# Hybrid decoder layer on one core: the gate and branch products turned round to 512 columns, with a clamp moved to ScalarE and a tile moved in SBUF

## The chip, the core and the metric

The kernel runs on one core of a Trainium2 chip. The metric is the device time of one execution in microseconds (us), the median of several runs. The profile names the engines as follows: PE is TensorE (matrix products) and PEld its weight loads, DVE is VectorE, ACT is ScalarE, POOL is GpSimd, and SP is SyncE, which here only issues DMAs. "L198" is line 198 of the kernel before.

## What is computed

The input is `x` with 256 tokens of 1024 channels. The layer is a SwiGLU feed-forward block, a mixer, and a second SwiGLU block, each with an RMSNorm in front and behind. The change lies in the mixer:

```python
u = rmsnorm(h, mix_pre_g)
z, xbc, dt_raw, q, k, v, gate_logits = jnp.split(u @ w_in, IN_SPLITS, axis=-1)
y_ssd = ssd_branch(z, xbc, dt_raw, ...)      # Mamba-2, ends in y @ ssd_w_branch  (2048 -> 1024)
y_att = diff_attn_branch(q, k, v, ...)       # ends in out @ da_w_branch          (1024 -> 1024)
gates = jax.nn.sigmoid(gate_logits + gate_b).reshape(b, L, 2, D_MODEL)
merged = gates[:, :, 0] * y_ssd + gates[:, :, 1] * y_att
h = h + rmsnorm(merged @ w_out, mix_post_g)
```

Inside `ssd_branch` the decay between two tokens of a chunk is `exp(a_cum[l] - a_cum[s])` for `s <= l` and zero otherwise. The kernel clamps the exponent at zero, so that the masked half can't overflow, and masks by a multiplication afterwards.

## The kernel before

**Precision and products.** Every large product is done in three: both operands are split into a rounded high part and the remainder (`hi`, `lo`, type fp32r), and hi·hi, hi·lo and lo·hi are summed in PSUM. Weights come in as chunks of 1 MB, listed at the top in the order of use (L86 to L132). `load_to` issues the loads on SP into three buffers `raw`. `split_steps` (L147) splits a chunk: ScalarE writes `whi` (L164) and VectorE `wlo` (L165), in four tiles. `take` (L177) hands out the next chunk and traces the splits of the chunks up to two ahead.

**Memory.** Most tiles of 4 KB a partition share one pool, `k4`, with 29 buffers. The normed input `u` has its own two buffers (tag `u8`). PSUM has eight banks: three for `pj`, the accumulators of products, and five for `bg`, used by everything smaller and by the four accumulators of a down projection (`acc_mx`, `acc_f`).

**Two forms of product.** `mm_t` (L191) keeps a 128x128 piece of the weights in the array and streams the 256 tokens, so the result has channels on partitions: 48 matmuls of 256 columns a chunk of 1024x256. `mm_nat` (L221) keeps 128 tokens of the activation in the array and streams 512 weight columns, so the result has tokens on partitions: 12 matmuls of 512 columns for a block of 128 tokens and a chunk of 512x512. Before the change the gates, both branches, and the projections to x, z, q and k use `mm_t`; V and the first columns of each feed-forward block use `mm_nat`. `mm_n` (L418) is the down projection: weights of 256 rows and 1024 columns, streamed 512 columns at a time, with the merged activations as stationary operand. Its first chunk is used at once for both token blocks, its last three are held and used block by block.

**Order.** From L1042 on PE runs in the order in which the program is written (`own_order(PE)`); the other engines are ordered by the framework's scheduler, in program order as far as operands are ready by its own model of time. `Background` (L976) feeds the smaller work between the large products: each generator yields what a step is priced at, `run(us)` adds to an account and issues steps until it is spent, and a `BREAK` ends a run. The steps are those of `ssd_work` (L769, the decays E and the products py), `ssd_norm` (L809) and `att_work` (L951, eight heads in four pairs; `Pair.turn`, L934, transposes a pair's output and splits it to `oh` and `ol`). Runs are placed after each product of z, q and k (`BG_US`, 2.8) and at each half chunk of the gates and of the SSD branch (`SLOT_US`, 1.55).

**The tail of the mixer.** Gates (L1047 to L1065): product, bias and eviction on ScalarE (L1056), then one switch of the activation table to the sigmoid and back. SSD branch (L1069 to L1077): product, VectorE multiplies by the gate (L1076). Attention branch (L1084 to L1105): the first chunk's product waits for three of four pairs, runs six of its eight K tiles, drains the background (with the last pair's transposes), and then goes on; VectorE multiplies by the gate and adds (L1096 to L1100); `split` writes `mh` and `ml`, which are already in the form in which `mm_n` wants them (channels on partitions). Then come `acc_mx` (L1107), `mm_n` (L1115) and the second feed-forward block.

Of the kernel before, what the change touches and what calls it, by code (L numbers as in the profile page):

```python
# [15 lines left out]
F32R = mybir.dt.float32r  # L16
# [22 lines left out]
WARM = 6  # L39
FILL = 8  # L40
TAIL = 3
BG_US = 2.8
SLOT_US = 1.55
BREAK, STOP = object(), object()


# [1 line left out]
def tile_hybrid_layer(ctx: ExitStack, tc: tile.TileContext, x, ffn1_pre_g, ffn1_w_gate, ffn1_w_up,  # L48
# [10 lines left out]
    def k4(shape, name, dt=F32):  # L59
        return sb.tile(shape, dt, tag="k4", name=name, bufs=K4_BUFS)  # L60
# [17 lines left out]
    def pjt(name):  # L78

        return pj(name).rearrange("p (m t) -> p m t", m=2)  # L80
# [7 lines left out]
    def t_chunk(w, k0, c0):  # L88
        chunks.append((w[k0:k0 + D, c0:c0 + T].rearrange("(j p) c -> p j c", p=P), [P, KD, T]))
# [30 lines left out]
    for c in range(4):  # L120
        t_chunk(w_in2, 0, Q0 + c * T)
        t_chunk(w_in2, 0, KK0 + c * T)
    for c in range(8):
        t_chunk(w_in2, 0, G0 + c * T)
    for c in range(4):
        t_chunk(ssd_w_branch[0], 0, c * T)
        t_chunk(ssd_w_branch[0], D, c * T)
    for c in range(4):
        t_chunk(da_w_branch[0], 0, c * T)
    for c in range(4):  # L130
        n_chunk(w_out[0], c * 2 * P)
    ffn_chunks(ffn2_w_gate, ffn2_w_up, ffn2_w_down)  # L132
# [55 lines left out]
        nc.scalar.copy(hi, src)  # L188
        nc.vector.tensor_sub(lo, src, hi.bitcast(F32))

    def mm_t(acc, w, act, k0=0, first=True, last=True, slot=None, ks=range(KD)):  # L191

        (wh, wl), (ah, al, _) = w, act
        acc = acc if isinstance(acc, list) else [acc[:, m, :] for m in range(2)]
        for m in range(2):
            cs = slice(m * P, (m + 1) * P)
            for j in ks:
                nc.tensor.matmul(acc[m], wh(j)[:, cs], ah(k0 + j), start=first and j == ks[0], stop=False)  # L198
                nc.tensor.matmul(acc[m], wh(j)[:, cs], al(k0 + j), start=False, stop=False)  # L199
            for j in ks:  # L200
                nc.tensor.matmul(acc[m], wl(j)[:, cs], ah(k0 + j), start=False, stop=last and j == ks[-1])  # L201
            if slot and m == 0:
                slot()

    def mm_w(dst, name, w, act):

# [45 lines left out]
    def own_order(*engines):  # L252

        if not ordered[0]:
            order_of[0].enter_context(tc.manual_schedule(engines=set(engines)))
            ordered[0] = True
# [43 lines left out]
    cols_a = const.tile([P, P], F32, name="cols_a")  # L300
    col, gain_rows = {}, []
    row = 0
    for name, v in (("mx", mix_pre_g), ("f2", ffn2_pre_g), ("gb", gate_b),
                    ("ng", ssd_norm_g), ("cb", ssd_conv_b), ("sg", da_subln_g)):
        n = v.shape[1] // P
        gain_rows.append((row, n, v))
        col[name] = row
        row += n
# [106 lines left out]
        nc.gpsimd.dma_start(pg, v[0].partition_broadcast(P))  # L415
        return pg

    def mm_n(acc, acts, ready, turned):  # L418


        n = len(acts) // 2
        held = []

        def one(i, w, parts):
            wh, wl = w
            for kt in range(2):
                ah, al = acts[2 * i + kt]
                for b, qs in parts:
                    ts = slice(b * P, (b + 1) * P)
                    for x_, w_ in ((ah, wh), (al, wh), (ah, wl)):  # L430
                        for q in qs:
                            nc.tensor.matmul(acc[b][q], x_[:, ts], w_(kt)[:, halves[q]],  # L432
                                             start=i == 0 and kt == 0 and x_ is ah and w_ is wh,
                                             stop=i == n - 1 and kt == 1 and w_ is wl)

        for i in range(n):
            w = take()
            if i < n - TAIL:
                one(i, w, ((0, (0, 1)), (1, (0, 1))))
            else:  # L440
                held.append((i, w))
        own_order(PE)
        for q in range(2):
            for i, w in held:
                one(i, w, ((0, (q,)),))
        ready(0)
        for q in range(2):
            for i, w in held:
                if q == 1 and i == n - TAIL:
                    turned()  # L450
                one(i, w, ((1, (q,)),))
        split_to(taken[0] + AHEAD)
        ready(1)
# [268 lines left out]
    nc.tensor.matmul(pac[:, 288:320], tri, av[:, 1, :], start=True, stop=True)  # L722
    nc.tensor.matmul(pac[:, 320:352], after_m, av[:, 0, :], start=True, stop=True)
    acT = k2([H_SSD, T], "acT")
    nc.scalar.copy(acT, pac[:H_SSD, :T])
    acs = const.tile([P, 3, H_SSD], F32, name="acs")
    nc.scalar.copy(acs, pac[:, 256:352].rearrange("p (a h) -> p a h", a=3))
    acd = dram.tile([H_SSD, T], F32, name="acd")
# [40 lines left out]
    def ssd_work(groups):  # L769
        for g in groups:  # L770
# [10 lines left out]
            for hf in range(2):  # L781
# [4 lines left out]
                for pr in range(2):  # L786
                    E = k3([P, 2, 3 * P], f"E{g}{hf}{pr}")
                    for i in range(2):
                        hd = r0 + pr * 2 + i
                        lh = pr * 2 + i  # L790
                        nc.vector.tensor_scalar(E[:, i, :P], acb[:, lh, P:], acs[:, 1, hd:hd + 1], 0.0,
                                                ALU.subtract, ALU.min)
                        nc.vector.tensor_scalar(E[:, i, P:T], acb[:, lh, :P], acs[:, 0, hd:hd + 1], 0.0,
                                                ALU.subtract, ALU.min)
                        act(E[:, i, T:], acb[:, lh, P:], AF.Exp, bias=acs[:, 2, hd:hd + 1])
                    act(E[:, :, :T], E[:, :, :T], AF.Exp)
                    nc.vector.tensor_tensor(E, E, cbm[g].unsqueeze(1).to_broadcast([P, 2, 3 * P]), ALU.mult)
                    c = hf * 2 + pr
                    for i in range(2):
# [115 lines left out]
    class Pair:  # L915
# [18 lines left out]
        def turn(self):  # L934
            hp = self.hp
            pt = bg([P, 4, P], f"pto{hp}")
            for i in range(4):
                nc.tensor.transpose(pt[:, i, :], self.o[:, i, :], ident)
            if hp % 2 == 0:
                oh[hp // 2] = k4([P, 4, T], f"oh{hp}", F32R)  # L940
                ol[hp // 2] = k4([P, 4, T], f"ol{hp}", F32R)
            o = (hp % 2) * 2
            turned_pairs[0] += 1
            hi, lo = (w[hp // 2][:, o:o + 2, :].rearrange("p i t -> p (i t)") for w in (oh, ol))
            pt = pt.rearrange("p i t -> p (i t)")
            nc.scalar.activation(hi, pt, AF.Identity, scale=g8)
            nc.vector.scalar_tensor_tensor(lo, pt, g8, hi.bitcast(F32), ALU.mult, ALU.subtract)

# [92 lines left out]

    own_order(PE)  # L1042

    def slot():
        back.run(SLOT_US)

    def gates(half):  # L1047
        tiles = []
        for c in range(4):
            if c % 2 == 0:  # L1050
                tiles.append(k4([P, 4, T], f"gt{half}{c}"))
            acc = pjt(f"pgt{half}{c}")
            mm_t(acc, take(), act_u, slot=slot)
            for m in range(2):
                n = col["gb"] + half * 8 + c * 2 + m
                nc.scalar.activation(tiles[-1][:, (c % 2) * 2 + m, :], acc[:, m, :], AF.Identity,  # L1056
                                     bias=cols_a[:, n:n + 1])
            slot()
        return tiles

    gt0, gt1 = gates(0), gates(1)
    act_table(SIGMOID)
    for t in gt0 + gt1:
        act(t, t, AF.Sigmoid)
    act_table(EXP_LN)  # L1065
    while yl[3] is None:
        back.run(0.1)
    act_y = (lambda j: yh[j // 4][:, j % 4, :], lambda j: yl[j // 4][:, j % 4, :], None)
    for c in range(4):  # L1069
        acc = [pj(f"pws{c}{m}")[:, :T] for m in range(2)]  # L1070
        mm_t(acc, take(), act_y, 0, True, False, slot)
        slot()
        mm_t(acc, take(), act_y, KD, False, True, slot)
        for m in range(2):
            t = gt0[c // 2][:, (c % 2) * 2 + m, :]
            nc.vector.tensor_tensor(t, acc[m], t, ALU.mult)  # L1076
        slot()  # L1077
    del act_y
    yh = yl = None
    while turned_pairs[0] < 3:  # L1080
        back.run(0.1)
    act_o = (lambda j: oh[j // 4][:, j % 4, :], lambda j: ol[j // 4][:, j % 4, :], None)

    w0, acc0 = take(), [pj(f"pwd0{m}")[:, :T] for m in range(2)]  # L1084
    mm_t(acc0, w0, act_o, 0, True, False, slot, range(6))
    slot()
    back.drain()
    act_table(SILU)
    mg = []
    for c in range(4):  # L1090
        acc = pjt(f"pwd{c}") if c else acc0
        mm_t(acc, w0 if c == 0 else take(), act_o, 0, c > 0, True, None, range(KD) if c else range(6, KD))
        cs = slice((c % 2) * 2, (c % 2) * 2 + 2)
        t0, t1 = gt0[c // 2][:, cs, :], gt1[c // 2][:, cs, :]
        if c:
            nc.vector.tensor_tensor(t1, acc, t1, ALU.mult)  # L1096
        else:
            for m in range(2):
                nc.vector.tensor_tensor(t1[:, m, :], acc[m], t1[:, m, :], ALU.mult)
        nc.vector.tensor_tensor(t1, t1, t0, ALU.add)  # L1100
        if c % 2 == 0:
            mh = k4([P, 4, T], f"mh{c}", F32R)
            ml = k4([P, 4, T], f"ml{c}", F32R)
        split(mh[:, cs, :], ml[:, cs, :], t1)
        mg += [(mh[:, cs.start + m, :], ml[:, cs.start + m, :]) for m in range(2)]  # L1105
    pg = load_gain(mix_post_g, "pg_mx")
    acc = [[bg([P, 512], f"acc_mx{b}{q}") for q in range(2)] for b in range(2)]  # L1107

# [3 lines left out]
        post_norm(b, acc[b], pg, 1.0, "mxp")  # L1112
        ready(b)

    mm_n(acc, mg, mixed, turned)  # L1115


    ov = out[0].rearrange("(b p) d -> p b d", p=P)
# [42 lines left out]
```

## Time and profile before

| | us |
|---|---|
| median of 3 runs (759.28 to 759.61) | 759.56 |
| the profiled execution, its time | 759.13 |
| the profiled execution, its span from the first to the last instruction | 757.4 |

| stretch of the span (us) | what runs in it on PE |
|---|---|
| 246 to 295 | x projection, with the convolution |
| 295 to 407 | z, q and k projections, with the decays, py and the SSD norm between |
| 407 to 461 | gates, with SSD norm and heads 0 to 3 between |
| 461 to 518 | SSD branch, with heads 4 to 7 between |
| 518 to 543.5 | attention branch |
| 543.5 to 566 | down projection `acc_mx` and the norm before the second feed-forward block |

Durations are those of one profiled execution. Consecutive matmuls overlap (their starts lie closer together than their listed durations), so their pace is read from the chain of work, where each piece is charged only with what it adds. A busy share of an engine is a sum of listed durations.

### The profile page before, as it was taken

Reading aid. Unit: us, or ns where it says so; the run is one execution under the profiler, and the core shown is the slowest. Engines: PE = TensorE matmul, PEld = TensorE weight load, DVE = VectorE, ACT = ScalarE, POOL = GpSimd, SP = SyncE. Lnnn points to the kernel's source line nnn. Section 1 sums busy time; section 2 is a strip of 40 time slices with the busy share of each in tenths; the row PEclk is TensorE's granted clock in tenths of the full one; section 3 lists DMA queues with packets and bytes.
Section 4 is the critical chain, followed back from the end, with each engine's and each line's share of the span. In section 5 each row is a group of like instructions: output and inputs, shape, how many; then the busy total and the mean of one; then the engine's idle time right before and its main releaser. Section 6 shows DMA issues by size and latency. Waiting matters only on the chain.

```text
span 757.4 us, 11973 instructions
## 1 busy us (share of the span) xinstructions
PE 746.9 (99%) x4841; PEld 670.7 (89%) x4841; DVE 524.0 (69%) x819; ACT 436.0 (58%) x716; POOL 39.0 (5%) x75
## 2 busy tenths in 40 slices
PE   8999999999999999999999999999999999999996
PEld 7888888888889999899999999999988888888885
DVE  6686567664577888887877866975884867766612
ACT  7465557553656565666846768654573756664511
POOL 6400000000200000000000000000010000000000
PEclk9999999999999999999999999999999999999999
DMA  9685666576253738465645663543671667544701
GB/s 319 156 280 158 212 222 245 188 263 221 63 167 114 223 117 269 146 221 173 189 117 163 189 201 112 177 156 114 222 250 56 222 223 221 169 172 184 283 0 56
DMA packets 104200, 136.99 MB, mean 181 GB/s; under 512 B 2668, under 2 KB 88784, under 8 KB 104144
## 3 DMA queue, kind: packets, MB, share of 16 engines
q1 hardware_dynamic: 101728, 129.51, 52.0%
q0 software_dynamic: 2112, 6.18, 2.7%
q8 instruction: 38, 0.62, 0.3%
q10 hardware_dynamic: 304, 0.53, 0.2%
q14 instruction: 18, 0.15, 0.1%
HBM read 135.13 MB, written 1.08 MB: 180 GB/s over the span
## 4 chain that ended last, share of the span: by engine, by line
PE 96%; DVE 1%; POOL 1%; ACT 1%; DMA 1%; issue 0%; SPq 0%; DVEq 0%; POOLq 0%; ACTq 0%
PE acc_f L432 16%; PE pup_f L215 9%; PE pg_f L215 9%; PE pn_f L230 5%; PE pg_f L214 4%; PE pup_f L214 4%; PE pn_mx L230 3%; PE acc_mx L432 3%; PE pws L198 2%; PE pgt L198 2%; PE pxs L201 2%; PE pws L201 2%; PE pxs L199 2%; PE pgt L201 2%; PE pxs L198 2%; PE pgt L199 2%
## 5 line engine op out<-in xcount | busy, mean ns | idle before, releaser
L165 DVE TENSOR_TENSOR wlo<-raw,whi 128x1024 fp32r<-128x1024 f32 (+1 forms) x246 | 291.9, 1214 | 50.0 <-ACT whi L164 49.1
L164 ACT CAST whi<-raw 128x1024 fp32r<-128x1024 f32 (+1 forms) x246 | 247.1, 1043 | 52.7 <-PE acc_f L432 19.9
L215 PE MATMUL pg_f<-u_f,whi 128*128 128x512 f32 x288 | 101.2, 396 | 0.0
L215 PE MATMUL pup_f<-u_f,whi 128*128 128x512 f32 x288 | 101.1, 396 | 0.0
L214 PE MATMUL pg_f<-u_f,wlo 128*128 128x256 f32 x252 | 70.5, 280 | 0.0
L214 PE MATMUL pup_f<-u_f,wlo 128*128 128x256 f32 x252 | 70.3, 279 | 0.0
L215 PEld LDWEIGHTS pg_f<-u_f,whi 128*128 128x128 f32 x288 | 52.9, 188 | 9.7
L215 PEld LDWEIGHTS pup_f<-u_f,whi 128*128 128x128 f32 x288 | 52.7, 188 | 9.8
L432 PE MATMUL acc_f<-whi,gh_f 128*128 128x512 f32 x176 | 58.1, 390 | 0.0
L432 PE MATMUL acc_f<-whi,gl_f 128*128 128x512 f32 x176 | 58.1, 389 | 0.0
L432 PE MATMUL acc_f<-wlo,gh_f 128*128 128x512 f32 x176 | 58.1, 389 | 0.0
L214 PEld LDWEIGHTS pg_f<-u_f,wlo 128*128 128x128 f32 x252 | 47.5, 189 | 1.7
L214 PEld LDWEIGHTS pup_f<-u_f,wlo 128*128 128x128 f32 x252 | 47.5, 189 | 1.6
L219 DVE TENSOR_TENSOR su_f<-pup_f,su_f 128x256 f32<-128x256 f32 x36 | 15.2, 422 | 40.0 <-ACT su_f L218 40.0
L432 PEld LDWEIGHTS acc_f<-wlo,gh_f 128*128 128x128 f32 x176 | 33.0, 188 | 6.9
L432 PEld LDWEIGHTS acc_f<-whi,gl_f 128*128 128x128 f32 x176 | 33.0, 188 | 6.9
L432 PEld LDWEIGHTS acc_f<-whi,gh_f 128*128 128x128 f32 x176 | 33.0, 188 | 6.7
L198 PE MATMUL pgt<-u_mx,whi 128*128 128x256 f32 x128 | 32.5, 291 | 0.0
L198 PE MATMUL pz<-u_mx,whi 128*128 128x256 f32 x128 | 32.3, 288 | 0.0
L198 PE MATMUL pws<-yh,whi 128*128 128x256 f32 x128 | 32.2, 290 | 0.0
L199 PE MATMUL pz<-u_mx,whi 128*128 128x256 f32 x128 | 31.7, 284 | 0.0
L198 PE MATMUL pxs<-u_mx,whi 128*128 128x256 f32 x128 | 31.7, 285 | 0.0
(311 smaller groups left out, 1571.9 us busy)
## 6 DMA issues: line engine op xcount, KB each, us to landing
raw<-in_w_in_dram SPq DMA_DIRECT2D x40, 1024.0 KB, 5.5
raw<-in_ffn_w_down_dram SPq DMA_DIRECT2D x22, 1024.0 KB, 5.4
raw<-in_ffn_w_gate_dram SPq DMA_DIRECT2D x20, 1024.0 KB, 5.9
raw<-in_ffn_w_up_dram SPq DMA_DIRECT2D x20, 1024.0 KB, 5.5
raw<-in_ssd_w_branch_dram SPq DMA_DIRECT2D x8, 1024.0 KB, 5.3
acb<-acd POOLq DMA_DIRECT2D x8, 512.0 KB, 4.3
raw<-in_da_w_branch_dram SPq DMA_DIRECT2D x4, 1024.0 KB, 5.3
raw<-in_w_out_dram SPq DMA_DIRECT2D x4, 1024.0 KB, 5.0
```

The costliest lines, as they stand in the source:

```text
L164: nc.scalar.copy(hi[:, js, :], r[:, q * nj + j:q * nj + j + n, :])
L165: nc.vector.tensor_sub(lo[:, js, :], r[:, q * nj + j:q * nj + j + n, :], hi[:, js, :].bitcast(F32))
L198: nc.tensor.matmul(acc[m], wh(j)[:, cs], ah(k0 + j), start=first and j == ks[0], stop=False)
L199: nc.tensor.matmul(acc[m], wh(j)[:, cs], al(k0 + j), start=False, stop=False)
L201: nc.tensor.matmul(acc[m], wl(j)[:, cs], ah(k0 + j), start=False, stop=last and j == ks[-1])
L214: nc.tensor.matmul(acc[:, :T], wl(j)[:, cs], ah(j), start=False, stop=False)
L215: nc.tensor.matmul(acc, wh(j)[:, cs], ahl(j), start=j == 0, stop=j == KD - 1)
L219: nc.vector.tensor_tensor(dst[:, m, :], acc[:, :T], dst[:, m, :], ALU.add)
L230: nc.tensor.matmul(acc, a(k0 + j), b(j), start=first and i == 0, stop=last and i == 11)
L432: nc.tensor.matmul(acc[b][q], x_[:, ts], w_(kt)[:, halves[q]], start=i == 0 and kt == 0 and x_ is ah and w_ is wh, stop=i == n - 1 and kt ...
```

## The change

Every part is in the mixer.

1. **The products turned round.** Gates, SSD branch and attention branch are computed by `mm_nat` through a new helper `natural`: two accumulators of 128 tokens by 512 channels, a chunk of 512x512 used for block 0 and block 1 in turn, a background run after each. The chunk lists become 512x512 pieces; number and bytes stay as they are.
2. **What follows from it.** The bias of the gates now lies along the free axis, so `gate_b` is broadcast to all partitions by two DMAs on GpSimd's queue (one small load of it at the start goes), and the eviction is an addition on VectorE. The sigmoid stays. Multiplications by the gate have 512 columns. The merged result has tokens on partitions and must be transposed for `mm_n`: `turn_merged` does 4 transposes on PE for each block and half, and splits from PSUM. The first half's are issued after the first chunk of the second half; the second half's inside `mm_n`, through a new argument `begun`, after its first chunk and ahead of the held three.
3. **The clamp.** `acT` is stored negated. For each head one of the two clamps (`tensor_scalar` on VectorE) becomes a `Relu` on ScalarE with the bias operand; the Exp takes scale -1.
4. **Half of `o`.** `oh` and `ol` of pairs 2 and 3 lie in one tile of the `u8` pool, free once the gates are done, in place of two `k4` tiles.
5. **The background's account.** `BG_US` 2.8 becomes 3.15; a run in the gates is worth 1.35; in the SSD branch 1.55 as before. The attention branch waits for two pairs, and drains after its first chunk.

```diff
-BG_US = 2.8
-SLOT_US = 1.55
+BG_US = 3.15
+GATE_US = 1.35
+SSD_US = 1.55
...
-    def mm_n(acc, acts, ready, turned):
+    def mm_n(acc, acts, ready, turned, begun=lambda: None):
...
         own_order(PE)
+        begun()
         for q in range(2):
...
-    nc.scalar.copy(acT, pac[:H_SSD, :T])
+    nc.scalar.activation(acT, pac[:H_SSD, :T], AF.Copy, scale=-1.0)
...
-                        nc.vector.tensor_scalar(E[:, i, :P], acb[:, lh, P:], acs[:, 1, hd:hd + 1], 0.0,
-                                                ALU.subtract, ALU.min)
+                        act(E[:, i, :P], acb[:, lh, P:], AF.Relu, bias=acs[:, 1, hd:hd + 1])
                         nc.vector.tensor_scalar(E[:, i, P:T], acb[:, lh, :P], acs[:, 0, hd:hd + 1], 0.0,
-                                                ALU.subtract, ALU.min)
-                        act(E[:, i, T:], acb[:, lh, P:], AF.Exp, bias=acs[:, 2, hd:hd + 1])
-                    act(E[:, :, :T], E[:, :, :T], AF.Exp)
+                                                ALU.add, ALU.max)
+                        act(E[:, i, T:], acb[:, lh, P:], AF.Exp, bias=acs[:, 2, hd:hd + 1], scale=-1.0)
+                    act(E[:, :, :T], E[:, :, :T], AF.Exp, scale=-1.0)
...
+            elif hp == 2:
+
+                o8 = sb.tile([P, 4, 2, T], F32R, tag="u8", name="o8", bufs=2)
+                oh[1], ol[1] = o8[:, :, 0, :], o8[:, :, 1, :]
...
+    def natural(name, n, hi, lo, evict, us, then=lambda: None):
+
+
+        accs = [pj(f"{name}{b}") for b in range(2)]
+        for i in range(n):
+            w = take()
+            for b in range(2):
+                bs = slice(b * P, (b + 1) * P)
+                mm_nat(accs[b], w, (lambda k: hi(k)[:, bs], lambda k: lo(k)[:, bs]), i * 4, i == 0, i == n - 1, "u")
+                if i == n - 1:
+                    evict(b, accs[b])
+                back.run(us)
+            if i == 0:
+                then()
+
+
+    gt = [[None] * 2 for _ in range(2)]
+    for half in range(2):
+        gb = k4([P, D], f"gb{half}")
+        nc.gpsimd.dma_start(gb, gate_b[0][half * D:(half + 1) * D].partition_broadcast(P))
+        for b in range(2):
+            gt[half][b] = k4([P, D], f"gt{half}{b}")
+        for q in range(2):
+            def gate(b, acc):
+                nc.vector.tensor_tensor(gt[half][b][:, halves[q]], acc, gb[:, halves[q]], ALU.add)
+
+            natural(f"pgt{half}{q}", 2, uh, ul, gate, GATE_US)
...
+        natural(f"pws{q}", 4, lambda j: yh[j // 4][:, j % 4, :], lambda j: yl[j // 4][:, j % 4, :], gated, SSD_US)
...
+    while turned_pairs[0] < 2:
         back.run(0.1)
...
+    def turn_merged(n):
+
+        for q, b, t, mh, ml in merges[:n]:
+            pt = bg([P, 4, P], f"pmg{q}{b}")
+            for m in range(4):
+                nc.tensor.transpose(pt[:, m, :], t[:, m * P:(m + 1) * P], ident)
+            bs = slice(b * P, (b + 1) * P)
+            split(mh[:, :, bs], ml[:, :, bs], pt)
+        del merges[:n]
+
+    def attended():
+        back.drain()
+        act_table(SILU)
...
+        def merge(b, acc):
+            t0, t1 = gt[0][b][:, halves[q]], gt[1][b][:, halves[q]]
             nc.vector.tensor_tensor(t1, acc, t1, ALU.mult)
...
+            nc.vector.tensor_tensor(t1, t1, t0, ALU.add)
+            merges.append((q, b, t1, mh, ml))
+
+        natural(f"pwd{q}", 2, lambda j: oh[j // 4][:, j % 4, :], lambda j: ol[j // 4][:, j % 4, :], merge,
+                SSD_US if q == 0 else 0.0, (attended, lambda: turn_merged(2))[q])
...
-    mm_n(acc, mg, mixed, turned)
+    mm_n(acc, mg, mixed, turned, lambda: turn_merged(2))
```

More of the change, by code (lines that the diff above doesn't have):

```diff
@@ L122, in tile_hybrid_layer @@
         t_chunk(w_in2, 0, KK0 + c * T)
-    for c in range(8):
-        t_chunk(w_in2, 0, G0 + c * T)
     for c in range(4):
[L126 to L129, printed above, removed]
+        for k0 in (0, 512):
+            s_chunk(w_in2, k0, G0 + c * 512)
+    for c in range(2):
+        for k0 in range(0, 2 * D, 512):
+            s_chunk(ssd_w_branch[0], k0, c * 512)
+    for c in range(2):
+        for k0 in (0, 512):
+            s_chunk(da_w_branch[0], k0, c * 512)
     for c in range(4):
@@ L189, in split, with mm_t @@
         nc.vector.tensor_sub(lo, src, hi.bitcast(F32))
-    def mm_t(acc, w, act, k0=0, first=True, last=True, slot=None, ks=range(KD)):
+    def mm_t(acc, w, act, k0=0, first=True, last=True, ks=range(KD)):
         (wh, wl), (ah, al, _) = w, act
@@ L201, in mm_t @@
                 nc.tensor.matmul(acc[m], wl(j)[:, cs], ah(k0 + j), start=False, stop=last and j == ks[-1])
-            if slot and m == 0:
-                slot()
     def mm_w(dst, name, w, act):
@@ L302, in tile_hybrid_layer @@
     row = 0
-    for name, v in (("mx", mix_pre_g), ("f2", ffn2_pre_g), ("gb", gate_b),
+    for name, v in (("mx", mix_pre_g), ("f2", ffn2_pre_g),
                     ("ng", ssd_norm_g), ("cb", ssd_conv_b), ("sg", da_subln_g)):
@@ L938, in turn @@
                 nc.tensor.transpose(pt[:, i, :], self.o[:, i, :], ident)
-            if hp % 2 == 0:
-                oh[hp // 2] = k4([P, 4, T], f"oh{hp}", F32R)
-                ol[hp // 2] = k4([P, 4, T], f"ol{hp}", F32R)
+            if hp == 0:
+                oh[0] = k4([P, 4, T], "oh0", F32R)
+                ol[0] = k4([P, 4, T], "ol0", F32R)
+            elif hp == 2:
+                o8 = sb.tile([P, 4, 2, T], F32R, tag="u8", name="o8", bufs=2)
+                oh[1], ol[1] = o8[:, :, 0, :], o8[:, :, 1, :]
             o = (hp % 2) * 2
             turned_pairs[0] += 1
-            hi, lo = (w[hp // 2][:, o:o + 2, :].rearrange("p i t -> p (i t)") for w in (oh, ol))
-            pt = pt.rearrange("p i t -> p (i t)")
+            hi, lo = (w[hp // 2][:, o:o + 2, :] for w in (oh, ol))
+            pt = pt.rearrange("p (i b) t -> p i (b t)", i=2)
             nc.scalar.activation(hi, pt, AF.Identity, scale=g8)
@@ L1042, in tile_hybrid_layer @@
     own_order(PE)
[L1044 to L1061, printed above, removed]
+    def natural(name, n, hi, lo, evict, us, then=lambda: None):
[20 more added lines that the diff above has]
+            natural(f"pgt{half}{q}", 2, uh, ul, gate, GATE_US)
     act_table(SIGMOID)
-    for t in gt0 + gt1:
+    for t in gt[0] + gt[1]:
         act(t, t, AF.Sigmoid)
@@ L1067, in tile_hybrid_layer, with gated @@
         back.run(0.1)
[L1068 to L1078, printed above, removed]
+    for q in range(2):
+        def gated(b, acc):
+            t = gt[0][b][:, halves[q]]
+            nc.vector.tensor_tensor(t, acc, t, ALU.mult)
+        natural(f"pws{q}", 4, lambda j: yh[j // 4][:, j % 4, :], lambda j: yl[j // 4][:, j % 4, :], gated, SSD_US)
@@ L1079, in tile_hybrid_layer @@
     yh = yl = None
-    while turned_pairs[0] < 3:
+    while turned_pairs[0] < 2:
         back.run(0.1)
[L1082 to L1095, printed above, removed]
-            nc.vector.tensor_tensor(t1, acc, t1, ALU.mult)
[L1097 to L1105, printed above, removed]
+    mg, merges = [], []
@@ new lines, in turn_merged @@
+    def turn_merged(n):
[9 more added lines that the diff above has]
+        act_table(SILU)
+    for q in range(2):
+        mh = k4([P, 4, T], f"mh{q}", F32R)
+        ml = k4([P, 4, T], f"ml{q}", F32R)
+        mg += [(mh[:, m, :], ml[:, m, :]) for m in range(4)]
+        def merge(b, acc):
+            t0, t1 = gt[0][b][:, halves[q]], gt[1][b][:, halves[q]]
+            nc.vector.tensor_tensor(t1, acc, t1, ALU.mult)
+            nc.vector.tensor_tensor(t1, t1, t0, ALU.add)
+            merges.append((q, b, t1, mh, ml))
+        natural(f"pwd{q}", 2, lambda j: oh[j // 4][:, j % 4, :], lambda j: ol[j // 4][:, j % 4, :], merge,
+                SSD_US if q == 0 else 0.0, (attended, lambda: turn_merged(2))[q])
```

## The prediction

> **What bounds the kernel now.** I read the page first, for the engine that is never idle and for the chain of work.
>
> ```profile
> span 757.4 us, 11973 instructions
> PE 746.9 (99%) x4841; PEld 670.7 (89%) x4841; DVE 524.0 (69%) x819; ACT 436.0 (58%) x716; POOL 39.0 (5%) x75
> ...
> PE 96%; DVE 1%; POOL 1%; ACT 1%; DMA 1%; issue 0%; SPq 0%; DVEq 0%; POOLq 0%; ACTq 0%
> ```
>
> PE makes up 96% of the chain. The second view is the list of PE's own waits, complete in these six rows (engine, what waited, whom for: us in total, times, longest).
>
> ```profile
> PE warm L293 <- POOL ident L279: 1.6, 1, 1.6
> PE pwd L198 <- ACT oh L946: 0.8, 1, 0.8
> PE pu_f L339 <- POOL un_f L372: 0.5, 1, 0.5
> PE pwd L199 <- DVE ol L947: 0.4, 1, 0.4
> PE pac L720 <- DVE av L716: 0.3, 1, 0.3
> PE py L802 <- DVE E L797: 0.2, 1, 0.2
> ```
>
> Outside the start there is one wait of any size in the part that the change touches: the attention branch waits for the last pair (`oh`, `ol`), 0.8 and 0.4 us. So a gain here is fewer microseconds of matmul or the end of that wait, and a loss is any new wait. The third view gives the stretches of the mixer (start:end, length, then busy us of PE, PEld, DVE, ACT, POOL, the granted clock, DMA share, GB/s).
>
> ```profile
> 295.00:352.00 57.00, 56.75 (x475) 53.28 (x474) 44.24 (x87) 34.18 (x58) 2.63 (x5) 1.00 0.63 198
> 352.00:407.40 55.40, 55.40 (x461) 51.83 (x460) 43.41 (x71) 35.56 (x53) 1.06 (x2) 1.00 0.60 186
> 407.40:460.90 53.50, 53.50 (x443) 51.53 (x442) 40.77 (x67) 36.90 (x73) 0.00 (x0) 1.00 0.43 139
> 460.90:518.10 57.20, 57.20 (x483) 55.30 (x481) 42.58 (x78) 39.30 (x80) 0.00 (x0) 1.00 0.51 166
> 518.10:543.50 25.40, 24.22 (x200) 23.79 (x199) 16.84 (x23) 12.29 (x16) 0.53 (x1) 1.00 0.41 146
> 543.50:566.20 22.70, 22.70 (x105) 18.86 (x105) 19.55 (x27) 15.96 (x30) 1.73 (x4) 1.00 0.81 277
> ```
>
> PE has no idle time from 407 to 518 us, VectorE is busy for three quarters of the mixer, DMA for about half. The pace of the two kinds of product is read from the chain in order of time (start, us added, what).
>
> ```profile
> 204.61 5.46 PE pn_mx L230 x24
> ...
> 409.67 0.96 PE pgt L201 x8
> ...
> 522.64 0.45 PE pto L938 x4
> 523.11 0.70 ACT oh L946
> 523.83 0.76 DVE ol L947
> ...
> 543.49 17.71 PE acc_mx L432 x78
> ```
>
> A matmul of 256 columns adds 0.96 / 8 = 0.120 us. One of 512 columns adds 5.46 / 24 = 0.2275 us in exactly the form that the change uses (L230), and 17.71 / 78 = 0.227 us in `mm_n`. Two narrow ones do the work of one wide one and take 0.240 us.
>
> **The change part by part.**
>
> *The products.* The counts come from the groups by line; L199 and L201 have as many as L198, since `mm_t` issues the three together.
>
> ```profile
> L198 PE MATMUL pgt<-u_mx,whi 128*128 128x256 f32 x128 | 32.5, 291 | 0.0
> L198 PE MATMUL pws<-yh,whi 128*128 128x256 f32 x128 | 32.2, 290 | 0.0
> L198 PE MATMUL pwd<-oh,whi 128*128 128x256 f32 x64 | 16.0, 286 | 0.8 <-ACT oh L946 0.8
> ```
>
> 3 x (128 + 128 + 64) = 960 narrow matmuls at 0.120 us, 115.2 us, become 480 wide ones at 0.2275 us, 109.2 us. That is **-6.0 us**, all on PE and so on the path.
>
> The Trainium skill, "TensorE: Matmul & The Clock Gate", section "Back-to-back issue gap", gives N / 2.4 + 2.5 ns between matmuls at full clock. By it 256 columns would take 109.2 ns and 512 columns 215.8, and this term would be 480 x 2.5 ns, only 1.2 us. The trace doesn't agree: 120 and 227.5 ns, at a granted clock of 1.00.
>
> *The merged transposes.* 16 of 128x128 are added on PE. The row for `pto` has four in 0.45 us, so 16 x 0.11 = **+1.8 us**.
>
> *The wait for the last pair.* I walked through the account by hand. Before, the last pair's transposes are issued between six and eight K tiles of the first attention product, and PE waits. After, 16 x 0.35 = 5.6 us more is spent before the gates, and these transposes are issued one block (12 x 0.2275 = 2.7 us) before the SSD branch ends, three blocks or 8.2 us ahead of the first product on `o8`; the copies take 0.70 + 0.76 us. The wait should go. It is worth 1.2 us by the two wait rows and about 1.7 by the chain (523.09, the end of `pto`, to the second product behind it); I take **-1.5**, between zero and 1.7. Next late is nothing that the trace shows: every other wait there is nil. `o8` takes a `u` buffer that the last gate product has left half a branch earlier.
>
> *The new wait in `mm_n`.* This is the term that I weigh most. At `begun` the four `acc_mx` tiles are being accumulated, so four of five `bg` banks are taken. Block 0's transposes take the fifth. Block 1's come next on PE and need a bank: they must wait until ScalarE and VectorE have both read block 0's. Everything of `mm_n` stands behind them in PE's own order. The price is the two copies and whatever those engines have ahead of them.
>
> ```profile
> L188 ACT CAST gh_f<-pt_f 128x512 fp32r<-128x512 f32 x4 | 2.3, 587 | 6.4 <-PE pt_f L534 6.4
> L189 DVE TENSOR_TENSOR gl_f<-pt_f,gh_f 128x512 fp32r<-128x512 f32 x4 | 2.8, 688 | 4.0 <-ACT gh_f L188 4.0
> ```
>
> ```profile
> 548.43 2.00 ACT L164 CAST whi<-raw 128x1024 fp32r<-128x1024 f32 x2 [1.12 <-DMA raw<-in_ffn_w_gate_dram]
> 551.33 2.00 ACT L164 CAST whi<-raw 128x1024 fp32r<-128x1024 f32 x2 [0.90 <-DMA raw<-in_ffn_w_gate_dram]
> ```
>
> ```profile
> 549.52 2.36 DVE L165 TENSOR_TENSOR wlo<-raw,whi 128x1024 fp32r<-128x1024 f32 x2
> 552.41 2.36 DVE L165 TENSOR_TENSOR wlo<-raw,whi 128x1024 fp32r<-128x1024 f32 x2 [0.54 <-ACT whi L164]
> ```
>
> Alone, the copies take 0.587 + 0.688 and about 0.1 between engines (the pair above: 523.09 to 524.59 for 0.70 + 0.76), 1.4 us. In today's clock `mm_n`'s first chunk ends at 543.49 + 24 x 0.227 = 548.9 and block 0's transposes at 549.4, in the middle of the split of the next block's first weights. Queued behind that split, VectorE begins at 551.9 and ends at 552.6: 3.2 us. Behind the second split as well: 554.8 + 0.7 = 555.5, 6.1 us. Zero would need a free bank, and there is none. With two `k4` buffers freed by `o8` the splits may run earlier than today. I take the middle of the two nearer ends, **+2.3 us**.
>
> *What is hidden.* Under PE's work lie the following.
>
> ```profile
> L791 DVE TENSOR_SCALAR E<-acb,acs 128x128 f32<-128x128 f32 x32 | 9.1, 284 | 0.0
> L244 ACT ACTIVATE E<-acb,acs 128x128 f32<-128x128 f32 x32 | 10.4, 393 | 0.8 <-PE py L803 0.8
> L1056 ACT ACTIVATE gt<-pgt,cols_a 128x256 f32<-128x256 f32 x16 | 6.7, 467 | 5.3 <-PE pgt L201 5.3
> L407 DVE TENSOR_TENSOR og_mxp<-acc_mx,pg_mx 128x512 f32<-128x512 f32 x4 | 2.8, 688 | 1.9 <-ACT jp_mxp L324 1.9
> pg_mx<-in_mix_post_g_dram POOLq DMA_DIRECT2D x1, 512.0 KB, 5.8
> POOL pg_mx L415 <- PE pwd L201: 165.9, 1, 165.9
> ```
>
> The clamp takes 9.1 us from VectorE and, at the price of its neighbour, the Exp of the same shape, gives ScalarE 32 x 0.393 = 12.6 us. From 295 to 407 us ScalarE goes from 69.7 to 82.3 of 112.4 us and VectorE from 87.7 to 78.6: both stay under PE, so nothing. The gates' eviction takes 6.7 us from ScalarE and gives VectorE 8 x 0.688 = 5.5 us; its accumulator is needed again two blocks (5.5 us) later at the earliest, so nothing while VectorE keeps up (a rival, below). The two broadcasts of 512 KB land in about 5.8 us and are needed 8.2 us after the gates begin; GpSimd's queue has been idle for 165.9 us by then. SP's queue has as many loads of 1 MB as before, in the same order. All of it costs nothing as long as PE is never starved.
>
> **Sum**: -6.0 - 1.5 + 1.8 + 2.3 = -3.4 us. The profiled execution took 759.13 (span 757.4, the rest outside it), 0.43 under the median 759.56; so 755.7 for its like, and **756.2** against the median.
>
> **The rivals.**
>
> *The bank is freed late.* ScalarE takes its work in a fixed order, and in program order the splits of two feed-forward chunks come ahead of this copy. Then the wait is 6.1 us in place of 2.3 and the sum +0.4: **760.0**, no change. For it: both splits waited for DMA in the rows above. Against: a sooner split with more `k4` free.
>
> *VectorE becomes the bound in the gates* (the slower side). Its stretch of 53.5 us shrinks by 192 x 0.0125 = 2.4 to 51.1 us, while VectorE's 40.8 us grow to 46.3. It is left 4.8 us of idle time and has 12.7 today. If its queue, stalled behind casts and exponents, needs more than 4.8 us, PE waits at the next head step in its own order. At today's idle time the stretch is 59.0 us, 7.9 longer: **764.1**. Against: idle time shrinks where work is waiting.
>
> *No gain from width.* If wide matmuls kept the narrow ones' pace per column (0.240 us), the first term would be zero: +2.6, **762.2**. Against: both wide rows. (The skill's rule above comes near to this, by an estimate 761.0.)
>
> *The clamp forces table loads.*
>
> ```profile
> L237 ACT ACT_TABLE_LOAD x9 | 11.5, 1283 | 1.5 <-PEq L1147 1.4
> ```
>
> The program asks for exactly nine, and all plain functions run without. Were Relu not in the Exp's table, 32 x 2 x 1.28 = 82 us of loads would take ScalarE's 82.3 us to 164 of 112.4, about 52 us more: **808**.
>
> **How the numbers follow.** Forecast 0.68; late bank 0.13; VectorE 0.12; no gain from width 0.06; table 0.01. The forecast's own range is 753.9 (no wait in `mm_n`) to 758.6 (a wait of 3.2 us and nothing from the last pair). I call 0.2%, 1.5 us, the least that a measurement of this kernel can tell from no change. Faster by more: 0.65, the forecast but for its upper end. Within: 0.16, that end and the late bank. Slower: 0.19, the other three. The range reaches to the late bank's upper end (with 1.2 us for the last pair), 753.9 to 760.3, and leaves out those three.
>
> **What would show it.** Products of `pgt`, `pws`, `pwd` at 0.2275 us a piece, 480 of them. No wait of PE for `oh` or `ol`. A wait of PE for `pmg` on VectorE's `ml`, once, of 1.4 to 3.2 us. PE waiting for `gt`, `s` or `aT` in the gates would bear out the slower rival. ACT_TABLE_LOAD x9 again. The prediction is wrong if PE is idle anywhere in the SSD part, or if the stretch from the gates to `acc_mx` (136.1 us today) isn't about 129.5 (-6.0, -1.5, and half of the transposes).

## The result and the profile after

The changed kernel takes 769.18 us (median of 4, 768.43 to 770.35) against 759.59, a ratio of 1.0129 with a 95% interval of 1.0111 to 1.0146. Forecast were 756.2 us and a gain. The profiled execution took 768.75 us, span 767.0.

The page of the changed kernel, with the lines that answer to those of before:

```profile
span 767.0 us, 11054 instructions
PE 747.7 (97%) x4377; PEld 649.0 (85%) x4377; DVE 522.1 (68%) x790; ACT 439.0 (57%) x732; POOL 39.9 (5%) x76
...
PE 92%; DVE 3%; ACT 2%; DMA 1%; POOL 1%; issue 1%; SPq 0%; DVEq 0%; POOLq 0%; ACTq 0%
```

PE has 464 instructions fewer, and yet is listed as busy for as long as before, in a span 9.6 us longer. VectorE and ScalarE take 3% and 2% of the chain where each had 1%. PE's own waits are a list of six again:

```profile
PE pmg L1098 <- DVE ml L192: 6.0, 1, 6.0
PE po L912 <- ACT aT L902: 3.8, 1, 3.8
PE warm L294 <- POOL ident L280: 1.6, 1, 1.6
PE pu_f L340 <- POOL un_f L373: 0.5, 1, 0.5
PE pac L722 <- DVE av L718: 0.3, 1, 0.3
PE py L803 <- DVE E L798: 0.2, 1, 0.2
```

The waits for `oh` and `ol` are gone. Two new ones have come: 6.0 us for the bank in `mm_n`, which was forecast at 2.3, and 3.8 us of head 3's values for `aT`, for which the sum had nothing. The stretches (columns as before) show where:

```profile
408.70:462.00 53.30, 53.30 (x269) 42.48 (x267) 44.80 (x75) 30.72 (x63) 0.53 (x1) 1.00 0.57 199
462.00:476.00 14.00, 10.16 (x46) 8.24 (x47) 6.62 (x13) 11.47 (x18) 0.00 (x0) 0.96 0.28 98
476.00:521.00 45.00, 45.00 (x228) 36.58 (x228) 38.31 (x61) 30.78 (x59) 0.00 (x0) 0.97 0.58 193
521.00:537.70 16.70, 16.70 (x78) 13.79 (x77) 5.23 (x8) 1.13 (x2) 0.53 (x1) 1.00 0.40 142
537.70:557.10 19.40, 13.36 (x66) 11.19 (x65) 16.95 (x18) 13.23 (x15) 0.00 (x0) 0.90 0.64 222
557.10:576.00 18.90, 18.90 (x82) 15.52 (x82) 8.59 (x17) 8.01 (x22) 1.74 (x4) 0.92 0.32 105
```

From the gates on PE is idle only at 462 to 476 and 538 to 557 us. The granted clock, 1.00 in every stretch of the mixer before, is below that there (0.96 and 0.90) and in the stretch behind each (0.97 and 0.92). In the chain of the changed kernel the cost of that is seen in the products:

```profile
476.09 3.84 PE pws L231 x12
...
521.35 16.38 PE pwd L231 x72
...
557.09 13.78 PE acc_mx L433 x54
```

Undisturbed, a wide product adds 16.38 / 72 = 0.2275 us, just as forecast. The twelve behind the first wait take 3.84 us in place of 2.7, the 54 behind the second 13.78 in place of 12.3.

**The first wait** is read from ScalarE's order in the changed kernel:

```profile
465.71 0.40 ACT L245 ACTIVATE s<-s,nm 128x128 f32<-128x128 f32 x1 [1.99 <-DVE nm L875]
...
467.60 1.28 ACT L238 ACT_TABLE_LOAD   x1
468.89 3.90 ACT L245 ACTIVATE gt<-gt 128x1024 f32<-128x1024 f32 x4
472.81 1.28 ACT L238 ACT_TABLE_LOAD   x1
474.10 0.48 ACT L902 COPY aT<-pa 128x384 f32<-128x384 f32 x1
```

The exponents of head 4 come first, since they need the Exp's table, then the switch, the gates' sigmoids, the switch back, and only then the copy `aT` of head 3. Its transposes on PE were done at 468.0 us, so the copy came 6.1 us late. PE runs on with products of the SSD branch, and then stands for 3.8 us, until 474.6. In the kernel before, the switch came ahead of head 4's exponents, with head 3's copy behind both, and PE didn't wait for that copy:

```profile
464.86 1.28 ACT L237 ACT_TABLE_LOAD   x1
...
470.07 1.28 ACT L237 ACT_TABLE_LOAD   x1
...
471.95 0.39 ACT L244 ACTIVATE s<-s,nm 128x128 f32<-128x128 f32 x1
...
474.64 0.47 ACT L901 COPY aT<-pa 128x384 f32<-128x384 f32 x1
```

**The second** is read from three engines, PE first, then ScalarE, then VectorE:

```profile
549.34 0.60 PE L1098 MATMUL pmg<-ident,gt 128*128 128x128 f32 x4
555.98 1.11 PE L1098 MATMUL pmg<-ident,gt 128*128 128x128 f32 x4 [6.04 <-DVE ml L192]
```

```profile
538.20 1.07 ACT L191 CAST mh<-pmg 128x512 fp32r<-128x512 f32 x2 [16.07 <-PE pmg L1098]
...
551.88 1.99 ACT L167 CAST whi<-raw 128x1024 fp32r<-128x1024 f32 x2 [2.28 <-DMA raw<-in_ffn_w_gate_dram]
553.78 0.58 ACT L191 CAST mh<-pmg 128x512 fp32r<-128x512 f32 x1
```

```profile
552.96 2.36 DVE L168 TENSOR_TENSOR wlo<-raw,whi 128x1024 fp32r<-128x1024 f32 x2 [1.13 <-ACT whi L167]
555.24 0.68 DVE L192 TENSOR_TENSOR ml<-pmg,mh 128x512 fp32r<-128x512 f32 x1
```

Block 0 was transposed by 549.9. Its copy stands on ScalarE behind the split of a gate chunk that itself waits 2.28 us for its DMA. And ScalarE had sat idle for 16.07 us before, waiting in its order for the first half's `pmg` when, as I read the order, it might have split the next chunk and so freed a raw buffer for that DMA (e9 tries this).

### The profile page after: what moved, and what is told of

It is laid out like the page before. It is cut to its first block, busy times and chain, and to the rows that moved or that the text cites. A ratio compares the mean times of both kernels' runs of the same rounds, so it can differ in the third digit from the quotient of the medians.

```text
span 767.0 us, 11054 instructions
## 1 busy us (share of the span) xinstructions
PE 747.7 (97%) x4377; PEld 649.0 (85%) x4377; DVE 522.1 (68%) x790; ACT 439.0 (57%) x732; POOL 39.9 (5%) x76
## 4 chain that ended last, share of the span: by engine, by line
PE 92%; DVE 3%; ACT 2%; DMA 1%; POOL 1%; issue 1%; SPq 0%; DVEq 0%; POOLq 0%; ACTq 0%
PE acc_f L433 16%; PE pup_f L216 9%; PE pg_f L216 9%; PE pgt L231 6%; PE pn_f L231 5%; PE pws L231 5%; PE pg_f L215 4%; PE pup_f L215 4%; PE pn_mx L231 3%; PE acc_mx L433 2%; PE pwd L231 2%; PE pxs L204 2%; PE pxs L202 2%; PE pxs L201 2%; PE pz L204 2%; PE pz L201 2%
## 5 line engine op out<-in xcount | busy, mean ns | idle before, releaser
L231 PE MATMUL pgt<-whi,u_mx 128*128 128x512 f32 x128 | 34.8, 400 | 0.0
L219 ACT COPY su_f<-pup_f 128x256 f32<-128x256 f32 x36 | 13.3, 370 | 32.0 <-PE pup_f L216 31.8
```

Source lines behind the costliest of these rows:

```text
L219: nc.scalar.copy(dst[:, m, :], acc[:, T:])
L231: nc.tensor.matmul(acc, a(k0 + j), b(j), start=first and i == 0, stop=last and i == 11)
```

## The experiments

The theory: the wide products bring what was forecast, and the whole loss is these two waits, each made by ScalarE's fixed order, with slow products behind them. The rivals: engines overloaded (then a wait returns elsewhere when one is removed), the bank alone, other parts of the change (clamp, tile in SBUF, form of the gates), and something else than idle time that slows the products.

| run | median us | ratio to before | 95% interval | largest waits of PE in the mixer |
|---|---|---|---|---|
| e1, sigmoids later | 762.75 | 1.0038 | 1.0025 to 1.0050 | 6.1 pmg |
| e2, other bank | 763.77 | 1.0051 | 1.0036 to 1.0066 | 3.8 aT, 1.4 pmg, 1.2 ml |
| e3, copies first | 762.76 | 1.0040 | 1.0025 to 1.0054 | 3.8 aT, 1.4 pmg |
| e4, account as before | 763.15 | 1.0044 | 1.0029 to 1.0059 | 5.9 pmg, 0.3 o |
| e7, e1 and e3 together | 755.96 | 0.9957 | 0.9945 to 0.9970 | 1.4 pmg |
| e5, e7 with the clamps back | 756.08 | 0.9956 | 0.9943 to 0.9968 | 1.4 pmg |
| e6, e7 with `o` in k4 | 755.96 | 0.9959 | 0.9945 to 0.9972 | 1.4 pmg |
| e9, split first | 764.42 | 1.0059 | 1.0045 to 1.0073 | 3.8 aT, 2.5 pmg |
| e10, e7, split first, other bank | 754.82 | 0.9937 | 0.9924 to 0.9951 | 0.2 wlo |
| e11, wait overfilled | 770.82 | 1.0151 | 1.0138 to 1.0165 | 3.8 aT |
| e12, account alone, on the kernel before | 764.05 | 1.0056 | 1.0042 to 1.0069 | 3.5 aT |
| e13, wait filled | 767.31 | 1.0106 | 1.0089 to 1.0123 | 3.8 aT, 0.6 pmg |

Where nothing else is said, the edit is made on the changed kernel.

**e1, the sigmoids behind the first SSD chunk.**

```diff
-    act_table(SIGMOID)
-    for t in gt[0] + gt[1]:
-        act(t, t, AF.Sigmoid)
-    act_table(EXP_LN)
...
-        natural(f"pws{q}", 4, ..., gated, SSD_US)
+        natural(f"pws{q}", 4, ..., gated, SSD_US, sigmoids if q == 0 else (lambda: None))
```

Here `sigmoids` holds the four lines that are taken out.

> The sigmoids of the gates are traced after the first chunk of the SSD branch instead of ahead of it; nothing else changes. Theory: the PE wait for aT (3.84 us) is ScalarE's order: head 3's copy aT stands behind two table loads and four sigmoids, which themselves wait for head 4's exponents. Then aT comes before the sigmoids, the wait goes, and with it the slow matmuls behind it (12 products in 3.84 us instead of 2.73): about -5 us, 764 us; the pmg wait stays at 6.0 us. Rival (ScalarE or VectorE is simply overloaded in the gates): a wait of the same size turns up at another head step, and the time stays near 769.

The `aT` wait is gone, and 6.4 us with it, where about 5 were expected. No other head step waits, so overloaded engines aren't the cause.

**e4 and e12, the account.** e4 gives the changed kernel the old account, e12 gives the kernel before the new one and nothing else.

```diff
-BG_US = 3.15
-GATE_US = 1.35
+BG_US = 2.8
+GATE_US = 1.55
```

> The background's account as before the change: 2.8 a product in z, q, k and 1.55 a block in the gates (16 blocks, as there were 16 half chunks). Walked through by hand, head 4's scores then come after the sigmoids are traced, and the last pair's transposes directly ahead of the product that reads them. If the account brought the aT wait, it goes (about -5 us) and the wait for oh and ol of about 1.5 us comes back: 765 to 766 us. If the broadcast gates or VectorE's eviction brought it, it stays: 769 to 771 us.

> The kernel before with the changed account alone (3.15 in z, q, k and 1.35 in the gates); narrow products, ScalarE's eviction of the gates, clamps on VectorE. Walked through by hand, head 4's scores then stand ahead of the sigmoids, as in the changed kernel. Theory (the account makes the aT wait, whatever the form of the products): a wait of PE for aT of 3 to 4 us with slow products behind it, 764 to 765 us. Rival (the wait needs the new form of the gates): no such wait, 759 to 760 us.

e12 has the wait in the narrow kernel, with ScalarE's eviction and both clamps on VectorE (its list of PE's waits):

```profile
PE po L912 <- ACT aT L902: 3.5, 1, 3.5
```

With e4, where it is gone, this shows that the account makes it: spending more before the gates brings head 4's scores ahead of the sigmoids. e12's 764.05 us lie within what was expected, e4's 763.15 below the 765 to 766. In e4 the last pair's wait comes back at 0.3 us, not at 1.5: in the wide form the first eight of a block's twelve products don't read the low part, so only the first copy is waited for.

**e2, another bank.** The transposes take their PSUM from `pj`.

```diff
-            pt = bg([P, 4, P], f"pmg{q}{b}")
+            pt = pj(f"pmg{q}{b}").rearrange("p (m t) -> p m t", m=4)
```

> The transposes of the merged result use a pj bank (free by then) instead of bg. Bank theory (the prediction's): the whole 6.0 us wait was for the bank, so it goes, with the slow matmuls behind it: about -8 us, 761 us. Order theory: the copy of block 0 is late by itself, because ScalarE and VectorE have the split of a chunk ahead of it that waits for its DMA; then block 1's transposes and six products (0.44 + 1.37 us) go on, and PE waits for ml at the products of chunk 2 instead: a wait of about 4.2 us, 766 to 767 us.

Neither number came: 763.8 lies between. The 6.0 us wait is gone, and two short ones stand in its place:

```profile
PE pmg L1098 <- DVE ml L192: 1.4, 1, 1.4
PE acc_mx L433 <- DVE ml L192: 1.2, 1, 1.2
```

The 1.4 us is at the first half, where the second half's accumulators still hold two of three `pj` banks, which I had overlooked. The 1.2 us is the late copy that the order theory asks for, but of 1.2 us rather than 4.2: in this order the second gate chunk is cast at 550.4 us, before block 0's transposes are done, and not 2 us behind them. So a free bank takes 3.4 us off the wait, though part of that is the changed order of the split.

**e3, the copies ahead of the splits.**

```diff
                 one(i, w, ((0, (0, 1)), (1, (0, 1))))
+                if i == n - TAIL - 1:
+                    begun()
...
         own_order(PE)
-        begun()
```

> The transposes and copies of the merged second half are traced right after the first chunk of the down projection, before the three held chunks are taken, so their copies stand ahead of the splits that those takes trace; PE's own order and the banks stay. Order theory: the pmg wait falls from 6.0 to 1.4 to 2 us and nothing runs slow behind it, 762 to 763 us. If a bank alone were the matter, the wait would stay near 6 us and the time near 769.

With the bank as scarce as before the wait is 1.4 us (its list of waits), the two copies and nothing else, and the products behind run at full pace:

```profile
PE pmg L1099 <- DVE ml L192: 1.4, 1, 1.4
```

**e9, the next chunk's split ahead of the first transposes.**

```diff
-(attended, lambda: turn_merged(2))[q])
+(attended, lambda: (split_to(taken[0] + AHEAD), turn_merged(2)))[q])
```

> Only one thing changes against the changed kernel: the split of the next chunk is traced ahead of the first merged transposes, so that ScalarE does it while it sat idle for 16.07 us on pmg; the copy in mm_n stays behind the split of two feed-forward chunks. Theory: the 6.0 us wait is a DMA that starts late because a raw buffer is freed late; with the buffer freed some 15 us sooner the second gate chunk lands about 4 us sooner, and the wait falls to 1.4 to 2.5 us: 762 to 764 us. Rival (the order of the copy behind two splits costs it whatever the DMA does): the wait stays above 4 us, 767 or more.

The wait falls to 2.5 us, the upper end, and the time to 764.4, just above it; the products behind the wait are still slow for a while. So without the raw buffer that ScalarE frees late 3.5 of the 6.0 us go; in the rest the copy still stands behind a split. The effects overlap: a free bank takes 3.4 us off the wait, the copy's place 4.6 and the earlier split 3.5, together more than there is. The wait needs the scarce bank and the late copy at once, and these figures are no shares of it.

**e7, both mends, and e5 and e6 on top of it.** e5 puts the clamp back to `tensor_scalar` (add, max) on VectorE; e6 puts `oh` and `ol` of pairs 2 and 3 back into `k4`.

> The sigmoids after the first SSD chunk and the copies of the merged second half ahead of the splits, together. If the two waits are the whole loss, and independent: 769.2 - 6.4 - 6.4 = about 756.4 us, 0.4% under the kernel before, with one pmg wait of 1.4 us left. If removing one only moves the work to the other: above 760.

> As the kernel with both mends, but both clamps on VectorE again. Theory (the clamp is hidden under PE's work either way): within 1.5 us of the kernel with both mends. Rival (VectorE needs the relief once the background is issued earlier): PE waits for E at py or for s and aT at the heads, and 3 us or more are lost.

> As the kernel with both mends, but the copies of pairs 2 and 3 lie in two tiles of k4 again. Theory (two tiles more or less do not bind, since PE waits for no split): within 1.5 us of the kernel with both mends. Rival (k4 is what limits how early the weights are split): PE waits for whi or ml around the down projection, 2 us or more lost.

e7 takes 755.96 us, 0.43% less than the kernel before, so the two waits add up and neither moves to another place. Clamp and tile make no difference that can be measured. In e5 VectorE is busy for 5.9 us more (527.0 against 521.1), and PE's waits for it are those of e7 to within 0.1 us.

**e10, no wait left.** e7 with e9's edit, and the second half's transposes alone in `pj`:

```diff
-            pt = bg([P, 4, P], f"pmg{q}{b}")
+            pt = bg([P, 4, P], f"pmg{q}{b}") if q == 0 else pj(f"pmg{q}{b}").rearrange("p (m t) -> p m t", m=4)
```

> Both mends, and the two things that still hold the copy up: the next chunk's split is traced ahead of the first merged transposes, and the second half's transposes use pj banks (free by then), so that block 1 need not wait for block 0's copies. If only the bank was left of the wait, 1.4 us go: 754.5 us, and no wait of PE over 0.6 us in the mixer. Rival: the wait moves to ml at the products of chunk 2 (1.8 us after block 0's transposes) and 1 us or more stays.

754.82 us, the fastest here, 0.63% less than the kernel before. The last of its five waits is the only one in the mixer behind the decays:

```profile
PE py L804 <- DVE E L799: 0.2, 1, 0.2
PE acc_mx L433 <- DVE wlo L168: 0.2, 1, 0.2
```

**e11 and e13, the wait filled with work.** Extra matmuls of a constant, whose result isn't used, between the two blocks' transposes; 50 in e11, 24 in e13.

```diff
+            if (q, b) == (1, 1):
+                pf = pj("fill")[:, :P]
+                for _ in range(24):
+                    nc.tensor.matmul(pf, ident, ident, start=True, stop=True)
```

> The changed kernel with 50 extra 128x128 matmuls of a constant into a free pj bank between the two blocks' transposes in mm_n (work that the result does not use); 50 x 0.11 = 5.5 us, so they fill most of the 6.0 us wait. Theory: the slow products behind the wait (54 in 13.78 us instead of 12.3, and four transposes in 1.11 instead of 0.45) come from PE's idle time, so they run at 0.2275 us here and the kernel gains about 2 us: 767 us. Rival (ScalarE and VectorE, busy with splits and copies at that moment, slow PE's reads): the products stay slow, and the time stays at 769.

> As the filled kernel, but with 24 extra matmuls: each turned out to be two PE instructions of 0.112 us, so 24 take 5.4 us and end inside the 6.0 us wait. Theory (the slow products come from PE's idle time): a wait of PE of 0.6 us or less, 54 products in 12.3 us and four transposes in 0.45 us, so 2.2 us less than the changed kernel, 767 us. Rival (something else slows them): 54 products in 13.8 us again and 769 us.

e11's filling took 11.2 us, twice what I had reckoned, and so cost more than the wait; but the 54 products behind it took 12.27 us. In e13 PE waits 0.6 us and the products take 12.29, as expected; the four transposes take 0.66 us, as behind the short wait of e7, and not the 0.45 expected. It is 1.9 us faster than the changed kernel with the same 6 us spent. The chain of e13:

```profile
556.24 0.66 PE pmg L1102 x4
556.90 12.29 PE acc_mx L433 x54
```

The granted clock from 556 to 562 us is 1.00. ScalarE and VectorE do the same work at that moment as in the changed kernel, so it is PE's idle time that makes the products slow.

## Why the prediction was wrong

To keep the start of the span out, which differs by up to 1.6 us between profiles of these kernels, I compare the stretch from the mixer norm's first transposes to the first product of the second feed-forward block: 375.75 us before, 384.44 after (+8.7), 372.44 in e7 (-3.3), 370.93 in e10 (-4.8).

- **The products, -6.0: right.** 0.2275 us a wide product, wherever PE isn't disturbed. From the first product of the gates to the first of `acc_mx` e7 takes 129.6 us against 135.9 before, 6.3 less where 6.6 were forecast. The rival "no gain from width" falls. So does the 1.2 us that was worked out by the formula of the Trainium skill, "TensorE: Matmul & The Clock Gate", section "Back-to-back issue gap"; the section gives it for an isolated matmul.
- **The merged transposes, +1.8: right.** Eight take 0.87 us in e3 and e7.
- **The last pair, -1.5: right**, the wait is gone.
- **The wait in `mm_n`, +2.3: the mechanism was right, the size was not.** It is 6.0 us, which I had worked out as the far end (6.1, behind both splits) and had given 0.13. I had read that splits stand ahead of the copy in program order, and then took the middle of the nearer ends on the hope that spare `k4` tiles would bring the splits forward. On top of e7, e6 shows that those tiles bind nothing; ScalarE sat idle for 16.07 us instead, waiting in order.
- **The step that failed outright is the account.** I followed 5.6 us more work ahead of the gates to the one place where it helps, the last pair, and dismissed the other steps with "every other wait there is nil". That was read from a trace in which they stood in another order. The account also moves head 4's scores ahead of the sigmoids' table switch, with head 3's copy behind it: 3.8 us of waiting (e1, e4, e12). PE waiting for `aT` had been named as a sign of the rival on the slower side, but that rival is an overloaded VectorE, and e1 ends the wait with the same work on VectorE. PE idle in the SSD part had been named as what would prove the prediction wrong, and that is what came.
- **Slow products behind a wait: not foreseen.** About 1.9 us behind the first (six products of `po` and twelve of `pws` in 5.3 us in place of the 3.4 of e1) and 2.2 behind the second (0.66 for the transposes, of which 0.2 also come behind the short wait of e7, and 1.5 for the 54 products).
- **Hidden: right** for the clamp (e5), the tile (e6), the broadcasts and the eviction of the gates.

The sum with the sizes as measured, where 8.2 is the second wait with its slow products and 5.7 the first with its own: -6.0 - 1.5 + 1.8 + 8.2 + 5.7 = +8.2 of the 8.7 us in the stretch; 0.5 is unaccounted for. Either of the two alone loses the gain: e1 and e3, which each leave one of them, take 762.8 us. That e7's 755.96 lies so near the forecast of 756.2 is luck in part: its wait in `mm_n` is 1.4 us and not 2.3, and some 0.8 us of its stretch are unaccounted for (-6.0 - 1.5 + 1.8 + 1.6 = -4.1, against -3.3; the 1.6 is the wait and the 0.2 behind it). Why the scheduler lets ScalarE wait for `pmg` rather than split the next chunk wasn't tried.

## What to carry to other kernels

When an engine with a fixed order is given work earlier, follow every step behind it on that engine, above all across a table switch, which gathers what comes before and holds up what comes after. Where PE is the bound, price a new wait not at the operation waited for but at everything ahead of it in that engine's order, DMA included, and add the slow products behind it (here none behind 1.4 us of waiting, 1.9 us behind 3.8 and 2.2 behind 6.0). Copies that PE will wait for belong ahead of prefetching work in the program.

## What the runs showed of the hardware

After PE had been idle for 2.5 to 6.0 us (e9, and both waits of the changed kernel), products of 512 columns came 0.427 us apart in place of 0.2275, and PE ran at this pace for some 3.3 to 4 us. PE in the changed kernel, two starts in the slow part and two behind it:

```profile
558.17 0.63 PE L433 MATMUL acc_mx<-whi,mh 128*128 128x512 f32 x1
558.60 0.63 PE L433 MATMUL acc_mx<-whi,ml 128*128 128x512 f32 x1
...
562.10 0.39 PE L433 MATMUL acc_mx<-whi,ml 128*128 128x512 f32 x1
562.33 0.39 PE L433 MATMUL acc_mx<-wlo,mh 128*128 128x512 f32 x1
```

PE in e9, from the end of the wait:

```profile
552.21 0.66 PE L1098 MATMUL pmg<-ident,gt 128*128 128x128 f32 x4 [2.54 <-DVE ml L192]
...
553.42 0.63 PE L433 MATMUL acc_mx<-wlo,mh 128*128 128x512 f32 x1
553.85 0.63 PE L433 MATMUL acc_mx<-whi,mh 128*128 128x512 f32 x1
```

The granted clock is 0.72 there (552 to 558 us). After 1.4 us (e3, e7) the products kept their pace, at a granted clock of 1.00; e7's chain:

```profile
544.70 0.66 PE pmg L1102 x4
545.35 12.27 PE acc_mx L433 x54
```

The Trainium skill, "TensorE: Matmul & The Clock Gate", section "What's actually happening", says that the array's clock falls to half after an idle window of about 3.4 us and comes back after a busy one. The half pace agrees (by an estimate from the section's 1.2 GHz, 512 columns take 426.7 ns), and so does the length of the slow part. The 2.5 us of e9 are less idle time than the section asks for. Counted from the last product ahead of the wait to the first behind it, with only transposes between, there are 3.4 us in e9 (549.2 to 552.6) and 2.3 in e7 (542.9 to 545.1); no run here shows whether transposes count as idle.

A 128x128 matmul of a plain fp32 constant is two instructions on PE, 100 of them in 11.17 us for 50 calls (e11), while a transpose of the same shape is one.
